# Block order, transpose placement, pairing and slot-table scatters in a fused decoder layer with 32 experts

## The chip, the cores and the metric

The kernel runs on one core of one Trainium2 chip. The metric is the device time of one execution in microseconds (us), lower is better. Shown are the median of three timed runs and one profiled execution.

## The reference, cut to what matters

One decoder layer for 1024 tokens of width 1024: a projection, banded attention and a convolution branch, their gated sum through `w_o`, a LayerNorm, and then a mixture of 32 experts of which each token takes four. The change touches the mixture alone:

```python
logits = h @ w_router + b_router
top_val, top_idx = lax.top_k(logits, TOP_K)         # 4 of 32
gates = softmax(top_val)
# the 4096 (token, expert) pairs are sorted by expert
for each expert e:
    up  = xb @ w_up[e] + b_up[e]                    # 1024 -> 2048
    act = min(glu, 7) * sigmoid(1.702 * glu) * (clip(lin, -7, 7) + 1)
    y  += gate * (act @ w_down[e] + b_down[e])      # 1024 -> 1024
x = layer_norm(alpha * h + y)
```

## The kernel before

**Dense part.** Up to about 640 us the kernel computes everything ahead of the experts. Its last loop runs over eight blocks of 128 tokens (lines 1120 to 1174): output projection, LayerNorm, router, top four, the rank of each token in its expert, and `place(b)` (line 1030), which writes for each of a token's four experts a record (token, gate) of 8 bytes into the slot table `tab` in HBM, by an indirect DMA from POOL. The token numbers of all records are written once (line 899). The framework orders two writes to `tab` by a wait for the first one's landing.

**Slot table and experts.** Experts are taken by rank of their token count; `CAPS` (line 52) gives each rank a fixed number of slots. A cap is cut into blocks of 128 (called F here), 64 and 32 slots: 320 is F, F, 64; 160 is F, 32; 96 is 64, 32. Tokens beyond a cap are counted by `overflow()` (line 1235, on DVE, called at slot 200) and worked off in a loop behind the last pair, which is skipped if there are none.

**Stages of an expert.** `fetch` reads its part of `tab`, `indices` turns it to integers, `gather` fetches the tokens' rows by indirect DMA into one of three buffers, and `x_T` (line 157) transposes them on TensorE (PE). A slot is a pair of weight tiles of 128 x 1024: slots 0 to 3 and 4 to 7 are the two halves of the up projection, 8 to 11 the down projection. `mm(s)` (line 233) runs the slot's products for every block, in order of the blocks. An F block takes 12 products of 128 x 512 a slot, each of high and low float32r parts of weights and inputs, which `split` (line 86) makes on ScalarE (ACT) and VectorE (DVE). Blocks of 64 and 32 take plain float32 products that use 64 or 32 columns of the array; in the trace each shows as two records. After slots 3 and 7 `swiglus` (line 281) adds the bias and applies the activation, on DVE and ACT, block by block. `act_T` (line 286) transposes the activations for the down projection. After slot 11 `scale_out` scales by the gate and `scatter` adds the rows to `yd` by indirect DMA. Sums stand in PSUM: five banks for sums (an F block takes two, a narrow one takes one) and three for transposes.

**Order of the work.** `PAIRS` (line 54) sets the order. A pair's slots interleave by fours: first expert 0 to 3, second 0 to 3, first 4 to 7, and so on, 24 slots a pair; the last pair runs one expert after the other. The list `G` holds all slots. The steps around them are put into a table `todo` by `at(slot, step)` (lines 1370 to 1409), and `behind(g)` (line 1411) issues those of slot g behind its products, in the order `rank_of`. `split_ahead` (line 1222) makes the high and low weights up to three slots ahead, and `load_ahead` loads weights from SP's queue as tile slots come free. POOL's queue carries, in program order, the scatters, table fetches, gathers and bias loads.

Of the kernel before, what the change touches and what calls it, by code (L numbers as in the profile page):

```python
# [15 lines left out]
ALU = mybir.AluOpType  # L16
# [7 lines left out]
NB = 8  # L24
# [25 lines left out]
BROW, BC, ACTB, XG = 2, 3, 3, 3  # L50
V_AT, S_AT = (2, 3, 4, 5, 7), (0, 3)
CAPS = [320, 288, 256, 256, 256, 256, 192, 192, 192, 160, 160, 160, 160, 128, 128, 128,
        128, 128, 128, 96, 96, 96, 96, 96, 96, 64, 64, 64, 64, 64, 64, 64]
PAIRS = [(6, 31), (1, 30), (13, 19), (2, 29), (9, 14), (7, 20), (21, 22), (0, 28), (15, 23), (3, 27), (10, 16), (8, 24),
         (11, 17), (4, 26), (12, 18), (5, 25)]
TR = 9 * P
FDVE = (0, 2, 5)

# [2 lines left out]
def kernel(ctx: ExitStack, tc: tile.TileContext, x, w_in, b_in, attn_sinks, w_attn_br,  # L61
# [39 lines left out]
    class Expert:  # L101
# [128 lines left out]
                        self.bias[u // 2, i, u % 2] = bc  # L230


        def mm(self, s, before=None):
            if s < 8 and s % 4 == 0 or s == 8:
                self.acc = [[acc(f"{self.pfx}{'d' if s == 8 else 'u'}{s}{i}{h}") for h in range(2 if w == P else 1)]
                            for i, (w, c) in enumerate(self.blocks)]
            raw, hi, lo = self.raw.pop(s), self.hi.pop(s, None), self.lo.pop(s, None)
            for i, (w, c) in enumerate(self.blocks):
                if before:
                    before(i)  # L240
                lhs = self.x[i] if s < 8 else self.aT[i]
                ng = P // w
                for kk in range(2):
                    k = 2 * (s % 4) + kk if s < 8 else 2 * (s - 8) + kk
                    st, sp = k == 0, k == KC - 1
                    if w == P and self.split:
                        terms = [(lhs[0], hi[kk]), (lhs[0], lo[kk]), (lhs[1], hi[kk])]
                    else:
                        terms = [(lhs[0], raw[kk])]
                    if w == P:  # L250
                        for h in range(2):
                            for j, (a, b) in enumerate(terms):
                                nc.tensor.matmul(self.acc[i][h], a[:, k, :], b[:, h * 512:(h + 1) * 512],
                                                 start=st and j == 0, stop=sp and j == len(terms) - 1)
                    else:
                        for j, (a, b) in enumerate(terms):
                            for g in range(ng):
                                if s < 8 and w == 32:
                                    rhs = b.rearrange("p (a f b t) -> p a b f t", a=2, b=2, t=2)[:, g // 2, g % 2]
                                else:  # L260
                                    rhs = b[:, g * 8 * w:(g + 1) * 8 * w]
                                nc.tensor.matmul(self.acc[i][0][g * w:(g + 1) * w, :8 * w], a[:, k, :], rhs,
                                                 start=st and j == 0, stop=sp and j == len(terms) - 1)
            wfree.extend(self.held.pop(s))

        def swiglu(self, v, i, h=0):
            w = self.blocks[i][0]
# [11 lines left out]
                                           op1=ALU.mult)  # L279

        def swiglus(self, v):
            for i, (w, c) in enumerate(self.blocks):
                for h in range(2 if w == P else 1):
                    self.swiglu(v, i, h)

# [49 lines left out]
    with ExitStack() as dctx:  # L335
# [559 lines left out]
        IDX = (rt.tile([P, NE, 4, 2], F32, name="slt"), rt.tile([P, NE, 4], I32, name="gi"),  # L895
               rt.tile([P, NE, 4], I32, name="si"))
        REC = wp.tile([P, NB, TOPK, 2], F32, name="rec", tag="rec", bufs=1)
        for b in range(NB):
            nc.gpsimd.tensor_scalar(REC[:, b, :, 0], prt.to_broadcast([P, TOPK]), float(b * P), None, op0=ALU.add)
        ids = rt.tile([1, NE], I32, name="ids")  # L900
        ids2 = rt.tile([1, NE], I32, name="ids2")
        nxi = rt.tile([1, 1], I32, name="nxi")
# [126 lines left out]

        def place(b):  # L1030
            for k in range(TOPK):
                nc.gpsimd.indirect_dma_start(out=tab[:, :], out_offset=bass.IndirectOffsetOnAxis(  # L1032
                    ap=DST[b][:, k:k + 1], axis=0), in_=REC[:, b, k, :], in_offset=None)

        def weigh(b):
            e4 = RG[b]
# [152 lines left out]
    with tc.manual_schedule():  # L1189
# [182 lines left out]

        blocks = [(e, i) for e in ex for i in range(e.nb)]
        g0 = {e.pfx: pos[e.pfx, 0] for e in ex}
        tpos = [g0[e.pfx] - 2 - e.nb + i for e, i in blocks]
        for n, e in enumerate(ex):
            p = g0[e.pfx] // 24 * 24
            if n > 1:
                at(p - 16, e.fetch)
                at(p - 13, e.indices)  # L1380
            for v in range(2):
                q = pos[e.pfx, 4 * v]
                at(min(q, g0[e.pfx] + 1) - 4 if e is last else q - 4, e.load_bias, v)
# [3 lines left out]
                at(q + 1, e.bias_of, 2 * v + 1)  # L1387
                at(q + 3, e.swiglus, v)
            for i in range(e.nb):
                at(pos[e.pfx, 4 + i], e.act_T, 0, i)  # L1390
                at(pos[e.pfx, 8 + (i > 0)], e.act_T, 1, i)
                if e is not last:
                    at(pos[e.pfx, 11], e.scale_out, i)
            if e is not last:
# [8 lines left out]
        for n, (e, i) in enumerate(blocks):  # L1403
            if n >= XG:
                f = g0[e.pfx] // 24 * 24
                at(max(tpos[n - XG], f - 12), e.gather, i)
        for n, (e, i) in enumerate(blocks):
            if e is not ex[0]:
                at(tpos[n], e.x_T, i)

        def behind(g):

            for f, a in sorted(todo.pop(g, ()), key=lambda fa: rank_of.index(fa[0].__name__)):
                f(*a)


        for g in range(FIRST):
# [13 lines left out]
        nc.vector.tensor_copy(bcol[:, 0, :], ccol[0:NE].to_broadcast([NE, P]))  # L1431
        for g, (e, s) in enumerate(G):
            split_ahead(g)
            e.mm(s, (lambda i: e.x_T(i) if i else None) if g == 0 else None)
            if g == 200:
                overflow()
            load_ahead(g)
# [65 lines left out]
```

## Time and profile before

| what | us |
|---|---|
| median of three runs | 2166.6 (2164.72 to 2170.33) |
| profiled execution | 2165.14 |
| its span on the core | 2163.5 |
| PE busy | 2064.2 |
| DVE busy | 1376.7 |
| ACT busy | 884.8 |
| POOL busy | 485.1 |

The span runs from the first instruction to the last. Busy time is the time in which an engine has at least one instruction at work; a list of waits gives the time in which it had none, with what ended each such time. The expert stage begins with the first transposes at 663.5 us. In the timeline a row has its start, its length, engine, line, operation, output <- inputs, the form of the array (rows * columns) and a count.

### The profile page before, as it was taken

The page shows a single profiled execution, that of the slowest core. Times are in us where ns is not written, and L with a number is a line of the kernel's source. Part 1 is how long each engine was busy: PE and PEld are TensorE (multiplying, and loading weights), DVE is VectorE, ACT ScalarE, POOL GpSimd, SP SyncE. Part 2 cuts the span into 40 slices and gives each one's busy share as a digit, 9 for nine tenths or more (in the row PEclk, how much of TensorE's full clock was granted, in tenths as well). Part 3 has the DMA queues.
Part 4 walks back from the last instruction along what each step waited for, and adds up shares of the span by engine and source line. Part 5 has one row for each costly group of instructions (what it writes and reads, how often), then busy time and mean ns, then how long its engine had stood idle before and what let it go on. Part 6 is the DMA issues. An engine that isn't in the chain of part 4 may idle for free. (4 is left out here: it accounts for less than half of the span.)

```text
span 2163.5 us, 31942 instructions
## 1 busy us (share of the span) xinstructions
PE 2064.2 (95%) x10929; PEld 1369.1 (63%) x10929; DVE 1376.7 (64%) x2058; ACT 884.8 (41%) x1356; POOL 485.1 (22%) x659
## 2 busy tenths in 40 slices
PE   7999999999977999999999999999999999999993
PEld 6776788887644566566664346556766456766771
DVE  3768799666765545654966134465678559649856
ACT  3155511432333424343653132333366346536633
POOL 1000000003324122322322332132141432322211
PEclk9999999999988999999999999999999999999997
DMA  6111011142237978998898997799889989997985
GB/s 199 42 39 30 20 54 54 44 133 62 99 136 261 334 262 296 376 349 302 276 313 298 341 362 248 263 321 374 306 263 316 329 264 323 346 313 259 333 288 214
DMA packets 191877, 510.84 MB, mean 236 GB/s; under 512 B 34844, under 2 KB 71118, under 8 KB 191709
## 3 DMA queue, kind: packets, MB, share of 16 engines
q1 hardware_dynamic: 162342, 446.76, 58.2%
q0 software_dynamic: 28816, 60.33, 10.9%
q8 instruction: 87, 1.43, 0.3%
q10 hardware_dynamic: 551, 1.66, 0.2%
q14 instruction: 81, 0.66, 0.1%
HBM read 473.08 MB, written 35.59 MB: 235 GB/s over the span
## 5 line engine op out<-in xcount | busy, mean ns | idle before, releaser
L611 DVE SCALAR_TENSOR_TENSOR c<-a,cw,c 128x1024 f32<-128x1024 f32 x120 | 154.0, 1284 | 3.3
L839 POOL DMA_DIRECT2D bu<-in_b_up_dram x2 | 1.0, 501 | 451.1 <-DVE wol L88 451.1
L141 POOL DMA_DIRECT2D slt<-tab x103 | 54.4, 529 | 30.4 <-issue 17.7
L91 PE MATMUL ga<-xh,whga 128*128 128x512 f32 x128 | 52.1, 407 | 0.0
L93 PE MATMUL ga<-xh,wlga 128*128 128x512 f32 x128 | 50.5, 395 | 0.0
L92 PE MATMUL ga<-xl,whga 128*128 128x512 f32 x128 | 50.5, 394 | 0.0
L93 PE MATMUL gb<-xh,wlgb 128*128 128x512 f32 x128 | 50.4, 394 | 0.0
L91 PE MATMUL gb<-xh,whgb 128*128 128x512 f32 x128 | 50.4, 394 | 0.0
L92 PE MATMUL gb<-xl,whgb 128*128 128x512 f32 x128 | 50.4, 394 | 0.0
L1032 POOL DMA_INDIRECT tab<-rec,dst x32 | 32.3, 1008 | 58.6 <-DMA tab<-rec,dst 55.8
L938 PE MATMUL wo<-woh,mh 128*128 128x512 f32 x128 | 36.9, 421 | 0.6 <-ACT mh L87 0.6
L938 PE MATMUL wo<-woh,ml 128*128 128x512 f32 x128 | 35.9, 404 | 0.0
L88 DVE TENSOR_TENSOR p7l<-p7w,p7h 128x1024 fp32r<-128x1024 f32 x24 | 29.5, 1279 | 9.6 <-ACT p7h L87 9.6
L88 DVE TENSOR_TENSOR p5l<-p5w,p5h 128x1024 fp32r<-128x1024 f32 x24 | 29.1, 1245 | 9.8 <-ACT p5h L87 9.1
L451 ACT ACTIVATE gt<-ga,pcol 128x512 f32<-128x512 f32 x16 | 11.0, 690 | 59.2 <-PE ga L93 59.1
L88 DVE TENSOR_TENSOR p8l<-p8w,p8h 128x1024 fp32r<-128x1024 f32 x24 | 28.5, 1241 | 10.1 <-ACT p8h L87 10.1
L654 DVE SCALAR_TENSOR_TENSOR sc<-s,mask 128x512 f32<-128x512 f32 (+1 forms) x32 | 19.5, 652 | 24.0 <-PE s L651 21.8
L88 DVE TENSOR_TENSOR p15l<-p15w,p15h 128x1024 fp32r<-128x1024 f32 x24 | 28.3, 1227 | 9.5 <-ACT p15h L87 9.4
L88 DVE TENSOR_TENSOR p13l<-p13w,p13h 128x1024 fp32r<-128x1024 f32 x24 | 29.0, 1257 | 8.4 <-ACT p13h L87 8.2
L88 DVE TENSOR_TENSOR p0l<-p0w,p0h 128x1024 fp32r<-128x1024 f32 x24 | 29.7, 1279 | 7.3 <-ACT p0h L87 7.1
L938 PE MATMUL wo<-wol,mh 128*128 128x512 f32 x128 | 33.9, 399 | 0.0
L88 DVE TENSOR_TENSOR p11l<-p11w,p11h 128x1024 fp32r<-128x1024 f32 x24 | 29.8, 1294 | 4.8 <-ACT p11h L87 4.6
(1271 smaller groups left out, 6373.0 us busy)
## 6 DMA issues: line engine op xcount, KB each, us to landing
p6w<-in_w_up_dram SPq DMA_DIRECT2D x16, 512.0 KB, 9.4
p31w<-in_w_up_dram SPq DMA_DIRECT2D x16, 512.0 KB, 8.3
p1w<-in_w_up_dram SPq DMA_DIRECT2D x16, 512.0 KB, 9.2
p30w<-in_w_up_dram SPq DMA_DIRECT2D x16, 512.0 KB, 5.4
p13w<-in_w_up_dram SPq DMA_DIRECT2D x16, 512.0 KB, 9.0
p19w<-in_w_up_dram SPq DMA_DIRECT2D x16, 512.0 KB, 13.2
p2w<-in_w_up_dram SPq DMA_DIRECT2D x16, 512.0 KB, 12.5
p29w<-in_w_up_dram SPq DMA_DIRECT2D x16, 512.0 KB, 11.5
```

The costliest lines, as they stand in the source:

```text
L88: nc.vector.tensor_tensor(lo, src, hi.bitcast(F32), op=ALU.subtract)
L91: nc.tensor.matmul(o, ah, bh, start=start, stop=False)
L92: nc.tensor.matmul(o, ah, bl, start=False, stop=False)
L93: nc.tensor.matmul(o, al, bh, start=False, stop=stop)
L141: nc.gpsimd.dma_start(self.m[g * w:(g + 1) * w, i, :], tab[bass.ds(row + c, w), :])
L451: nc.scalar.activation(GT[c][:, sl], t, AF.Sigmoid, bias=bin_c(14 + c))
L611: nc.vector.scalar_tensor_tensor(C[c], A[c][:, w:w + S], cw[:, c, w:w + 1], C[c], op0=ALU.mult, op1=ALU.add)
L654: nc.vector.scalar_tensor_tensor(SC[b][c0 // 2][:, g::2, :W], t[g][:, :, :W], 0.125, mk[:, None, :].to_broadcast([P, 2, W]), op0=ALU.mult, ...
L839: nc.gpsimd.dma_start(bu, b_up[:, i * S:(i + 1) * S])
L938: nc.tensor.matmul(t, ml[:, k, :], W[k][:, sl], start=n == 0, stop=n == 3 * KC - 1)
L1032: nc.gpsimd.indirect_dma_start(out=tab[:, :], out_offset=bass.IndirectOffsetOnAxis(ap=DST[b][:, k:k + 1], axis=0), in_=REC[:, b, k, :], in ...
```

## The change

The cap of rank 24 falls from 96 to 64. The pairs are chosen anew. In `mm` odd slots run the blocks in reverse; `between` lets the transposes due at an even slot run where it goes from F to narrow blocks. `swiglus` takes the blocks in reverse. Transposes of inputs move 3 slots earlier for the first expert of a pair; those of activations go to slots 5 and 8, and for a second expert without an F block 2 slots earlier. `fetch`, `indices` and `gather` move 4 to 5 slots earlier. `place` writes the token numbers itself, record by record, and its scatters are declared free of order among themselves.

```diff
 CAPS = [320, 288, 256, 256, 256, 256, 192, 192, 192, 160, 160, 160, 160, 128, 128, 128,
-        128, 128, 128, 96, 96, 96, 96, 96, 96, 64, 64, 64, 64, 64, 64, 64]
-PAIRS = [(6, 31), (1, 30), (13, 19), (2, 29), (9, 14), (7, 20), (21, 22), (0, 28), (15, 23), (3, 27), (10, 16), (8, 24),
-         (11, 17), (4, 26), (12, 18), (5, 25)]
+        128, 128, 128, 96, 96, 96, 96, 96, 64, 64, 64, 64, 64, 64, 64, 64]
+PAIRS = [(6, 31), (1, 30), (13, 19), (2, 29), (9, 14), (3, 28), (10, 15), (0, 27), (21, 22), (4, 26), (8, 20), (16, 23),
+         (11, 17), (7, 24), (12, 18), (5, 25)]
...
-        def mm(self, s, before=None):
+        def mm(self, s, before=None, between=None):
...
-            for i, (w, c) in enumerate(self.blocks):
+            order = list(range(self.nb))[::-1 if s % 2 else 1]
+            for n, i in enumerate(order):
+                w, c = self.blocks[i]
+                if between and n and s % 2 == 0 and w < P and self.blocks[order[n - 1]][0] == P:
+                    between()
+                    between = None
...
             wfree.extend(self.held.pop(s))
+            return between
...
         def swiglus(self, v):
-            for i, (w, c) in enumerate(self.blocks):
+            for i, (w, c) in reversed(list(enumerate(self.blocks))):
...
-        for b in range(NB):
-            nc.gpsimd.tensor_scalar(REC[:, b, :, 0], prt.to_broadcast([P, TOPK]), float(b * P), None, op0=ALU.add)
...
         def place(b):
             for k in range(TOPK):
-                nc.gpsimd.indirect_dma_start(out=tab[:, :], out_offset=bass.IndirectOffsetOnAxis(
+                nc.gpsimd.tensor_scalar(REC[:, b, k, 0:1], prt, float(b * P), None, op0=ALU.add)
+
+                i = nc.gpsimd.indirect_dma_start(out=tab[:, :], out_offset=bass.IndirectOffsetOnAxis(
                     ap=DST[b][:, k:k + 1], axis=0), in_=REC[:, b, k, :], in_offset=None)
+                tc.declare_no_dep(i.ins, group="place", reason="every token has a slot of its own")
+                tc.add_to_no_dep_group("place", i.ins)
...
-        tpos = [g0[e.pfx] - 2 - e.nb + i for e, i in blocks]
+        tpos = [g0[e.pfx] - (5 if n % 2 == 0 and n else 2) - e.nb + i for n, e in enumerate(ex) for i in range(e.nb)]
...
             if n > 1:
-                at(p - 16, e.fetch)
-                at(p - 13, e.indices)
+                at(p - 21, e.fetch)
+                at(p - 17, e.indices)
...
             for i in range(e.nb):
-                at(pos[e.pfx, 4 + i], e.act_T, 0, i)
-                at(pos[e.pfx, 8 + (i > 0)], e.act_T, 1, i)
+
+                d = -2 if n % 2 and e is not last and e.full == 0 else 0
+                at(pos[e.pfx, 4] + (d or (1 if e.nb > 1 else 0)), e.act_T, 0, i)
+                at(pos[e.pfx, 8] + (d or 0), e.act_T, 1, i)
...
-                at(max(tpos[n - XG], f - 12), e.gather, i)
+                at(max(tpos[n - XG], f - 16), e.gather, i)
...
-        def behind(g):
-
-            for f, a in sorted(todo.pop(g, ()), key=lambda fa: rank_of.index(fa[0].__name__)):
-                f(*a)
+        def behind(g, of=lambda f: True):
+
+            fs = sorted(todo.pop(g, ()), key=lambda fa: rank_of.index(fa[0].__name__))
+            todo[g] = [fa for fa in fs if not of(fa[0].__name__)]
+            if not todo[g]:
+                del todo[g]
+            for f, a in fs:
+                if of(f.__name__):
+                    f(*a)
...
-            e.mm(s, (lambda i: e.x_T(i) if i else None) if g == 0 else None)
+            between = e.mm(s, (lambda i: e.x_T(i) if i else None) if g == 0 else None,
+                           lambda: behind(g, lambda name: name in ("x_T", "act_T")))
+            if between:
+                between()
```

## Rows read from the trace of the kernel before

**Rows 1.** The page, busy us (share of the span) and instructions.

```profile
PE 2064.2 (95%) x10929; PEld 1369.1 (63%) x10929; DVE 1376.7 (64%) x2058; ACT 884.8 (41%) x1356; POOL 485.1 (22%) x659
```

**Rows 2.** Waits of PE: waiter <- releaser, us in total, times, longest.

```profile
PE fsp L1350 <- DVE fmvs L1348: 25.5, 1, 25.5
PE p6xt L167 <- DMA p6xg<-hd,gi: 20.0, 1, 20.0
PE p15u L253 <- DVE p15l L88: 4.5, 1, 4.5
...
PE p9d L253 <- DVE p9al L88: 0.8, 1, 0.8
```

**Rows 3.** Timeline of PE, pair (2, 29): first product of a plain run, and its end.

```profile
945.74 0.50 PE L253 MATMUL p2u<-p2h,p2xh 128*128 128x512 f32 x1
...
956.85 0.65 PE L262 MATMUL p29u<-p29w,p29xr 128*64 128x512 f32 x2
```

**Rows 4.** Timeline of PE, pair (6, 31): narrow and plain runs in turn.

```profile
681.59 1.94 PE L262 MATMUL p6u<-p6w,p6xr 128*64 128x512 f32 x8
683.46 0.50 PE L253 MATMUL p6u<-p6h,p6xh 128*128 128x512 f32 x1
...
686.44 1.94 PE L262 MATMUL p6u<-p6w,p6xr 128*64 128x512 f32 x8
...
695.18 0.50 PE L253 MATMUL p6u<-p6h,p6xh 128*128 128x512 f32 x1
```

**Rows 5.** Timeline of PE, pair (21, 22): three slots of 64 and 32 lie between.

```profile
1256.28 0.65 PE L262 MATMUL p22u<-p22w,p22xr 128*64 128x512 f32 x2
...
1264.97 0.39 PE L298 MATMUL p21aT<-ident,p21act 128*128 128x128 f32 x1
```

**Rows 6.** Timeline of PE, pair (21, 22): transposes between narrow products.

```profile
1278.16 1.09 PE L167 MATMUL p0xt<-ident,p0xg 128*128 128x128 f32 x8
```

**Rows 7.** Timeline of DVE and PE around the overflow count, pair (15, 23).

```profile
1436.11 0.18 DVE L1241 TENSOR_TENSOR over<-scnt_ps,capr 128x32 f32<-128x32 f32 x1
...
1442.53 0.17 DVE L1267 CAST xci<-xcol 128x2 int32<-128x2 f32 x1
...
1444.48 0.80 PE L253 MATMUL p15u<-p15l,p15xh 128*128 128x512 f32 x1 [4.48 <-DVE p15l L88]
...
1449.47 0.77 PE L262 MATMUL p23u<-p23w,p23xr 128*64 128x512 f32 x2
```

**Rows 8.** Window behind that wait: us, busy by engine, PEclk, DMA share, GB/s.

```profile
1444.50:1449.40 4.90, 4.90 (x11) 3.49 (x11) 2.06 (x3) 0.24 (x1) 0.00 (x0) 0.50 0.82 97
```

**Rows 9.** Timeline of DVE and POOL at the end of the dense part.

```profile
637.78 0.16 DVE L1027 SCALAR_TENSOR_TENSOR dst<-tif,rk 128x4 int32<-128x4 f32 x1
...
642.68 0.98 POOL L1032 DMA_INDIRECT tab<-rec,dst  x1 [5.76 <-DMA tab<-rec,dst]
...
651.66 0.97 POOL L1032 DMA_INDIRECT tab<-rec,dst  x1 [1.40 <-DMA tab<-rec,dst]
654.06 1.75 POOL L141 DMA_DIRECT2D slt<-tab  x3 [1.43 <-DMA tab<-rec,dst]
```

**Rows 10.** Windows by pair, (13, 19), (9, 14), (21, 22): PE, PEld, DVE, ACT, POOL.

```profile
859.64:933.96 74.32, 74.18 (x481) 42.00 (x479) 48.42 (x68) 35.18 (x50) 26.46 (x35) 1.00 1.04 373
1026.74:1115.30 88.56, 86.56 (x524) 62.08 (x523) 81.27 (x104) 58.20 (x75) 26.10 (x34) 1.00 0.85 290
1211.50:1288.93 77.43, 77.43 (x649) 27.14 (x645) 18.81 (x43) 14.95 (x31) 24.52 (x35) 1.00 1.04 353
```

**Rows 11.** Timeline of DVE, expert 0: the first operations of two halves of swiglu.

```profile
1314.69 0.69 DVE L272 TENSOR_TENSOR p0t<-p0u,p0bc 128x512 f32<-128x512 f32 x1 [17.67 <-PE p0u L253]
...
1316.73 0.69 DVE L272 TENSOR_TENSOR p0t<-p0u,p0bc 128x512 f32<-128x512 f32 x1
```

**Rows 12.** Waits of POOL, and what DVE's addition of p21's bias waited for.

```profile
POOL p13xg L154 <- DVE si L148: 33.2, 1, 33.2
...
  DMA p21bg<-bud: 9.3, 1
```

## The prediction

> **What bounds the kernel now.** I read the busy times first: TensorE (PE) is busy for 95% of the span [rows 1], so the next question is what it waits for. The list of its waits has few entries [rows 2]: 20.0 us for the first gather of the expert stage, 4.5 us in expert p15, and sub-microsecond waits on VectorE (DVE). (The 25.5 us at the end belong to the closing normalisation, which the change leaves alone.) From 663.5 us on PE simply works through its list, so there a change is worth what it takes off PE's list, wherever no other engine is close behind. So I then read the PE timeline for what one instruction costs and what a change of form costs (form: the shape in which the array is used, 128 output columns, 64, 32, or a transpose over 64 or 32 rows), and the stretches by pair of experts for who is close behind.
>
> **Prices.** In a plain run 48 products of 128 columns take 956.85 - 945.74 = 11.11 us [rows 3], 0.2315 each, 2.78 per slot of 12. Between narrow runs the same 12 take 686.44 - 683.46 = 2.98 [rows 4]: 0.20 more. A run of 8 narrow 64-column records (a float32 product shows as two) takes 1.87, and 40 take 8.74, so 32 more cost 6.87, 0.215 each; 8 alone would be 1.72, so a run carries 0.15 [rows 4]. Going to the narrow form and back costs 0.20 + 0.15 = 0.35, **0.175 us a change**. A slot of an expert with a 64 and a 32 block takes 8.69 / 3 = 2.90 [rows 5]; without 1.72 for its 64 block the 32 block and its two changes are 1.18, the block alone 0.83.
>
> **The change, part by part.**
>
> *Expert 24 loses its 32 block* (cap 96 to 64). 12 slots x 0.83 = 10.0 us, and some 1 us for 8 + 2 small transposes (an estimate: eight large ones take 1.09 [rows 6]). Its loads, scatter and 12 small DMAs lie beside other work. Gain 11. Tokens over a cap would run an extra pass after the last pair; the reference's routing sends 57 tokens to the 25th expert, so 64 suffice.
>
> *Turned order.* Odd slots run their blocks backwards, so F N, F N, F N, F N becomes F N, N F, F N, N F. I counted the changes of form between the matrix products from the two lists of pairs: before, pair by pair, 23, 27, 27, 6, 25, 44, 48, 24, 27, 6, 25, 44, 25, 5, 25, 1, together 382; after 17, 18, 18, 6, 13, 5, 13, 17, 24, 6, 30, 18, 13, 17, 13, 1, together 229. For example p9 (F and 32) beside p14 (F): 8 changes a phase become 4. 153 x 0.175 = 26.8 us.
>
> *Transposes.* A transpose of 128 rows is of the F form; inside a narrow run it costs two more changes. The partner's activations now go into the first expert's slots (2 slots earlier), the inputs 3 slots earlier. Counted the same way with the transposes in, the changes are 483 before and 293 after: 37 beyond the 153. 37 x 0.175 = 6.5 us. With x_T move its gather (16 instead of 12 slots ahead), the fetch of the slot table (21 for 16) and the index conversion (17 for 13): POOL issues the same instructions, now ahead of one phase more of bias loads. Their cost on PE is nothing as long as PE has products to run and the bias still comes in time; if not, each late microsecond is PE's (rival below). SP's weight loads keep their order; slots come free as before.
>
> *New pairs.* Slot 200, at which the overflow count is made, falls into the pair (21, 22) instead of (15, 23). The count keeps DVE from 1436.11 to 1442.7, with a weight split queued behind it; PE then waits 4.48 us, and the next 12 products take 1449.47 - 1444.48 = 4.99 instead of 2.78 [rows 7], at a granted clock of 0.50, the lower of the two levels, 1.2 GHz [rows 8]. (21, 22) has no F block and no split, so nothing is queued behind the chain: 4.5 + 2.2 = 6.7 us gained.
>
> *Scatters without order.* The last block's destinations are ready at 637.94, but its first scatter is issued at 642.68 and the fourth at 651.66, each after the one before has landed; the fetch follows at 654.06 [rows 9]. Unordered, each costs POOL 0.97 of issue and, as an estimate, 0.6 for the new small operation ahead of it and the semaphore: four are out by 644.4. A landing took 1.4 us in quiet and up to 5.8 beside the first weight loads [rows 9]; I take 2.5, nearer the quiet end since those loads are ending. Fetch at 647, 7 us earlier, and all that follows with it (fetch, indices, gather, first transpose) as PE has nothing else to do. Bounds 0 and 9. The order of the earlier blocks' scatters frees POOL only where PE doesn't wait for it.
>
> *Given back.* (a) In the four pairs of two F experts DVE is busy 81.3 of 88.6 us while PE is 86.6 [rows 10], and PE already waits for DVE there [rows 2]. 12 changes fewer, 2.1 us, put PE's need at 84.5 with DVE's unchanged, and DVE may split only three slots ahead; in the two up phases DVE is behind. I keep a third: -1.4 x 4 = -5.6 (bounds 0 and -8.4). (b) swiglus now takes the narrow block first and block 0 last. Experts 0 and 1 have three blocks and fill all five accumulator banks, so the partner's first product needs block 0's bank. One half takes DVE 1316.73 - 1314.69 = 2.04 [rows 11]; after the narrow block PE needs 2.98 + 2.78 = 5.8 to the end of the slot, and DVE comes to block 0 after three halves, from 0.1 + 2.0, then (waiting for block 1's first half) from 2.5 + 4.0 = 6.5, and frees the bank with its 0.7 us addition at 7.2: 1.4 us of wait, twice a pair, two pairs, 5.6. Should the pool hand out the bank that is released first, it is 0; with the same at the down phase 7. I take -5, nearest to what the round order of five banks gives. (c) (13, 19) and (21, 22) run at a DMA share of 1.04 [rows 10], so transfers can become late there: -1.
>
> **Sum.** 11 + 26.8 + 6.5 + 6.7 + 7 - 5.6 - 5 - 1 = 46.4. The profiled execution took 2165.1 (span 2163.5, 1.6 around it); the median of the runs is 2166.6, 1.5 above. 2165.1 - 46.4 = 2118.7, with the 1.5 added **2120 us**. About 0.3%, 6.5 us, is what a measurement of this kernel can tell from no change.
>
> **Rivals.**
>
> *Nothing is given back.* DVE and the banks keep up: 2120 - 11.6 = 2108. For it: DVE waits in the profile are under 1 us each [rows 2]; against it DVE's 92% in four pairs [rows 10].
>
> *Transfers pace the narrow pairs.* At 373 and 353 GB/s the engines of the narrow pairs are full [rows 10]; if PE was only just fed, (13, 19), (21, 22) and the new (16, 23) keep their lengths and lose what I gave them: 9, 24 and 9 changes x 0.175 and some 1 us of transposes each, 10 us, and DVE the rest of (a): 2120 + 10 + 2.8 = 2133. For it: share 1.04. Against: no wait of PE for a raw weight is in the list.
>
> *Slower: a late bias.* POOL works in order. Gathers now stand in the slot in which the second expert's bias is asked for, and a gather waits for indices: 33.2 us once [rows 12]. A bias row has already made DVE wait 9.3 us for p21 [rows 12], which cost PE nothing, since the partner's phase of 4 x 2.90 = 11.6 us covers it. From there each further microsecond stops PE for want of a bank. With the bias 16 us late in each of 15 pairs it would be 15 x 4.4 = 66: 2186. Against it: the second expert's bias is needed 7 slots, over 19 us, after it is asked for.
>
> *Slower: the clock.* Transposes now stand together, up to 13 in one slot. If such a batch let the clock fall, each would cost what the fall after the wait in p15 cost, 2.2 us [rows 7]; two batches a pair, 32 x 2.2 = 70: 2190. Against it: ten transposes in a row (8 at 1278.16 [rows 6], then 2) lie in a stretch with a granted clock of 1.00 [rows 10]. The Trainium skill, in "TensorE: Matmul & The Clock Gate", Part 4: PE-mode transpose, says that transposes do not count as PE activity in the way matmuls do, by which the batches could bring the clock down; the stretch just named does not agree.
>
> *The change doesn't do what it says.* If the scatters still wait for each other (through the tile they read, which is now written between them), the 7 us stay: 2127.
>
> **How the numbers follow.** Forecast 0.62 (2110 to 2129), nothing given back 0.15, transfers 0.13, scatters still ordered or little gained 0.05 (0.01 of it within 0.3%), late bias 0.03, clock 0.02. Faster 0.94, same 0.01, slower 0.05. The range, 2104 to 2136, takes in the bounds of the front (0 to 9), of (a) and (b), and the transfer case.
>
> **What would show it.** Right: narrow runs twice as long in p6 to p12; no wait in the ninth pair; last scatter and fetch 2 to 3 us apart, the first wait of PE near 13 us; the partners' 64 blocks without transposes inside their runs; (9, 14) shorter by about 1 us only; a wait of 1 to 1.5 us at the first products of p30 and p27. Wrong: PE waits for raw weights or for bias in the list, a clock below 1.00 between 700 and 2050 us, or plain F products slower than 0.23.

## The result and the profile after

| what | before | after |
|---|---|---|
| median of the runs, us | 2166.39 (2164.72 to 2170.33) | 2142.24 (2138.92 to 2142.89) |
| ratio, 95% interval | | 0.9883 (0.9869 to 0.9897) |
| span of the profiled execution | 2163.5 | 2141.3 |

The changed kernel is faster by 24 us, 1.2%; forecast were 46 and a time from 2104 to 2136. The direction was right, the size was not, and the time lies outside the range. (One execution of an experiment's kernel, e7, took 4305 us and is left out of its time below.) In the profiled executions the gain is 2163.5 - 2141.3 = 22.2 us. It has three parts, read one after the other: the front, the expert stage and the end.

The busy times, the packets of the software queue (q0; 28816 before) and the table fetches (103 before) on the page of after:

```profile
PE 2029.4 (95%) x10727; PEld 1377.7 (64%) x10727; DVE 1372.5 (64%) x2049; ACT 881.0 (41%) x1350; POOL 508.2 (24%) x669
...
q0 software_dynamic: 28240, 59.80, 11.1%
...
L141 POOL DMA_DIRECT2D slt<-tab x99 | 60.7, 876 | 15.0 <-DMA yd<-p15ys,gi 5.1
```

PE is busy 34.8 us less than before [rows 1], more than the 22.2 gained: some of its work went and idle time came. **The front**, timeline of DVE, POOL and PE:

```profile
635.37 0.16 DVE L1033 SCALAR_TENSOR_TENSOR dst<-tif,rk 128x4 int32<-128x4 f32 x1
...
639.53 1.06 POOL L1040 DMA_INDIRECT tab<-rec,dst  x1 [0.28 <-POOL rec L1038]
...
641.13 1.06 POOL L1040 DMA_INDIRECT tab<-rec,dst  x1 [0.28 <-POOL rec L1038]
...
645.22 1.74 POOL L141 DMA_DIRECT2D slt<-tab  x3 [3.03 <-DMA tab<-rec,dst]
...
653.73 1.94 PE L167 MATMUL p6xt<-ident,p6xg 128*128 128x128 f32 x8 [11.86 <-DMA p6xg<-hd,gi]
```

The last scatters are 1.6 us apart and wait only for the small operation ahead of them, not for a landing [rows 9]; the fetch stands at 645.22 instead of 654.06, and PE's wait for the first gather falls from 20.0 to 11.9 [rows 2]. The first transposes come 9.8 us earlier, at 653.73 instead of 663.48. Of these, 2.4 lie ahead of the scatters: the last block's destinations are ready at 635.53 instead of 637.94 [rows 9]. **The expert stage**, list of PE's waits:

```profile
PE fsp L1360 <- DVE fmvs L1358: 24.0, 1, 24.0
...
PE p6xt L167 <- DMA p6xg<-hd,gi: 11.9, 1, 11.9
PE p10aT L306 <- DVE p0xl L88: 6.7, 1, 6.7
...
PE p6aT L306 <- DVE p1xl L88: 2.0, 1, 2.0
...
PE p18u L260 <- ACT p18h L87: 1.6, 1, 1.6
...
PE p16d L260 <- ACT p16ah L87: 1.2, 1, 1.2
```

The 4.5 us for p15l are gone; two new waits stand in front, both of the activations' transposes for a split of *inputs* (p0xl, p1xl). The timeline of PE, DVE and ACT around the longer one:

```profile
1258.31 1.03 PE L167 MATMUL p0xt<-ident,p0xg 128*128 128x128 f32 x8
1259.18 0.64 PE L306 MATMUL p10aT<-ident,p10act 128*128 128x128 f32 x4
1259.42 0.68 DVE L280 TENSOR_TENSOR p15t<-p15u,p15bc 128x512 f32<-128x512 f32 x1
...
1262.39 2.00 ACT L87 ACTIVATE p10h<-p10w 128x1024 fp32r<-128x1024 f32 x2
...
1263.48 2.36 DVE L88 TENSOR_TENSOR p10l<-p10w,p10h 128x1024 fp32r<-128x1024 f32 x2
1264.28 1.07 ACT L87 ACTIVATE p0xh<-p0xt 128x512 fp32r<-128x512 f32 x2
...
1265.76 1.28 DVE L88 TENSOR_TENSOR p0xl<-p0xt,p0xh 128x512 fp32r<-128x512 f32 x2
1266.50 0.48 PE L306 MATMUL p10aT<-ident,p10act 128*128 128x128 f32 x1 [6.68 <-DVE p0xl L88]
1266.90 3.64 PE L269 MATMUL p10d<-p10w,p10ar 128*32 128x256 f32 x32
...
1278.45 1.92 PE L269 MATMUL p10d<-p10w,p10ar 128*32 128x256 f32 x30
```

The slot has four groups of transposes to do: two of x_T for expert 0 (two tiles of four), act_T of p10's F block and of its 32 block. There are three banks for transposes. The first three groups go through, the fourth needs a bank, and the bank is freed by the splits of p0's inputs, which stand on ACT and DVE behind p15's activation and p10's weight split. PE stands still for 6.68 us, and the narrow run behind it takes 3.64 where one of the same kind takes 1.92: the granted clock is 0.50 there, in a window just behind the wait:

```profile
1266.50:1270.50 4.00, 4.00 (x34) 1.56 (x34) 3.37 (x4) 2.17 (x3) 0.00 (x0) 0.50 0.34 79
```

Windows by pair of after, columns as in [rows 10]:

```profile
655.50:745.33 89.83, 86.67 (x394) 46.03 (x393) 51.45 (x72) 39.09 (x53) 25.92 (x34) 0.97 0.97 341
...
849.89:926.13 76.24, 73.76 (x481) 42.58 (x479) 46.77 (x66) 33.80 (x47) 25.48 (x34) 1.00 1.04 360
1018.34:1106.32 87.98, 85.77 (x524) 65.16 (x523) 80.92 (x102) 58.19 (x75) 23.43 (x28) 0.98 0.87 289
1198.36:1294.58 96.22, 87.88 (x532) 65.41 (x531) 81.68 (x103) 58.91 (x76) 33.95 (x33) 0.95 0.84 275
1409.88:1484.05 74.17, 73.39 (x627) 27.75 (x623) 23.23 (x76) 12.92 (x28) 19.87 (x29) 1.00 1.03 344
1671.51:1748.49 76.98, 74.74 (x480) 43.47 (x478) 46.10 (x64) 33.33 (x47) 29.34 (x41) 0.98 1.02 355
1835.65:1917.32 81.67, 81.67 (x378) 43.38 (x376) 46.50 (x64) 33.85 (x47) 22.75 (x30) 1.00 1.03 370
```

In order (6, 31), (13, 19), (9, 14), (10, 15), (21, 22), (16, 23), (7, 24). The first, second and fourth became longer than before (87.8, 74.3 and, for (10, 16), 88.7), (7, 24) is 15.8 shorter than (7, 20). **The end**, the last row of the timeline, after and then before:

```profile
2124.25 1.02 POOL L1371 DMA_INDIRECT out_dram<-yg,si  x1 [29.84 <-DVE yg L1368]
```

```profile
2157.30 1.03 POOL L1361 DMA_INDIRECT out_dram<-yg,si  x1 [30.12 <-DVE yg L1358]
```

It ends at 2125.27, the span at 2141.3: 16.0 us later. Before, the same row ended at 2158.33 and the span at 2163.5, 5.2 us later. So the last scatter came 33.1 us earlier, and 10.9 of these were lost behind it, where no view shows an instruction. The packed trace has two long records there, both of POOL: one named INC_SWDGE_SEM takes 2.69 us, 0.54 before, and the closing drain 10.20, 1.45 before. Together they are 10.9 longer, which is the whole loss.

### The profile page after: what moved, and what is told of

It is laid out like the page before. It is cut to its first block, busy times and chain, and to the rows that moved or that the text cites. A ratio compares the mean times of both kernels' runs of the same rounds, so it can differ in the third digit from the quotient of the medians.

```text
span 2141.3 us, 31584 instructions
## 1 busy us (share of the span) xinstructions
PE 2029.4 (95%) x10727; PEld 1377.7 (64%) x10727; DVE 1372.5 (64%) x2049; ACT 881.0 (41%) x1350; POOL 508.2 (24%) x669
## 5 line engine op out<-in xcount | busy, mean ns | idle before, releaser
L141 POOL DMA_DIRECT2D slt<-tab x99 | 60.7, 876 | 15.0 <-DMA yd<-p15ys,gi 5.1
L88 DVE TENSOR_TENSOR p16l<-p16w,p16h 128x1024 fp32r<-128x1024 f32 x24 | 29.3, 1261 | 18.7 <-ACT p16h L87 18.6
L1040 POOL DMA_INDIRECT tab<-rec,dst x32 | 36.6, 1143 | 15.5 <-POOL rec L1038 8.5
L88 DVE TENSOR_TENSOR p10l<-p10w,p10h 128x1024 fp32r<-128x1024 f32 x24 | 29.7, 1295 | 14.9 <-ACT p10h L87 14.8
L88 DVE TENSOR_TENSOR p8l<-p8w,p8h 128x1024 fp32r<-128x1024 f32 x24 | 28.5, 1242 | 15.8 <-ACT p8h L87 15.7
L88 DVE TENSOR_TENSOR p1l<-p1w,p1h 128x1024 fp32r<-128x1024 f32 x24 | 28.6, 1242 | 15.3 <-ACT p1h L87 15.2
L88 DVE TENSOR_TENSOR p9l<-p9w,p9h 128x1024 fp32r<-128x1024 f32 x24 | 28.8, 1257 | 14.2 <-ACT p9h L87 14.1
L88 DVE TENSOR_TENSOR p13l<-p13w,p13h 128x1024 fp32r<-128x1024 f32 x24 | 28.8, 1239 | 14.2 <-ACT p13h L87 14.1
L88 DVE TENSOR_TENSOR p12l<-p12w,p12h 128x1024 fp32r<-128x1024 f32 x24 | 28.8, 1258 | 13.1 <-ACT p12h L87 12.9
L88 DVE TENSOR_TENSOR p2l<-p2w,p2h 128x1024 fp32r<-128x1024 f32 x24 | 28.2, 1222 | 12.8 <-ACT p2h L87 12.4
L88 DVE TENSOR_TENSOR p4l<-p4w,p4h 128x1024 fp32r<-128x1024 f32 x24 | 28.2, 1222 | 12.9 <-ACT p4h L87 10.9
```

The costliest lines, as they stand in the source:

```text
L88: nc.vector.tensor_tensor(lo, src, hi.bitcast(F32), op=ALU.subtract)
L141: nc.gpsimd.dma_start(self.m[g * w:(g + 1) * w, i, :], tab[bass.ds(row + c, w), :])
L1040: i = nc.gpsimd.indirect_dma_start(out=tab[:, :], out_offset=bass.IndirectOffsetOnAxis(ap=DST[b][:, k:k + 1], axis=0), in_=REC[:, b, k, :] ...
```

## The experiments

Lengths of the pairs in the profiled executions, from the first product of one pair to that of the next (us; before's partner in brackets where it differs; the kernels are told of below):

| pair | before | after | e2 | e3 | e5 | e9 |
|---|---|---|---|---|---|---|
| (6, 31) | 87.8 | 89.8 | 85.6 | 86.9 | 87.0 | 90.9 |
| (1, 30) | 106.6 | 104.6 | 104.6 | 106.2 | 106.5 | 105.7 |
| (13, 19) | 74.3 | 76.2 | 75.5 | 75.0 | 73.6 | 76.3 |
| (2, 29) | 92.8 | 92.2 | 92.2 | 92.8 | 92.8 | 92.2 |
| (9, 14) | 88.7 | 88.0 | 87.3 | 86.9 | 87.1 | 87.4 |
| (3, 28) [3, 27] | 92.8 | 92.0 | 92.0 | 92.7 | 92.6 | 92.0 |
| (10, 15) [10, 16] | 88.7 | 96.2 | 88.4 | 88.9 | 90.1 | 98.8 |
| (0, 27) [0, 28] | 116.7 | 115.3 | 115.3 | 116.9 | 116.8 | 116.0 |
| (21, 22) | 76.0 | 74.2 | 74.3 | 74.2 | 73.9 | 76.3 |
| (4, 26) | 92.6 | 92.2 | 92.2 | 92.9 | 92.8 | 92.2 |
| (8, 20) [8, 24] | 97.7 | 95.2 | 95.2 | 96.2 | 96.3 | 97.5 |
| (16, 23) [15, 23] | 82.2 | 77.0 | 77.7 | 76.7 | 75.4 | 77.8 |
| (11, 17) | 88.9 | 87.2 | 87.4 | 87.9 | 90.1 | 89.8 |
| (7, 24) [7, 20] | 97.5 | 81.7 | 81.7 | 82.8 | 82.9 | 82.7 |
| (12, 18) | 88.7 | 88.3 | 87.7 | 87.8 | 89.2 | 90.5 |

**e1, the scatters alone**: the edit of `place` from the diff above, in the kernel before.

> The kernel before with the slot table's scatters unordered and nothing else. In the changed kernel the first transposes of the expert stage start 8.9 us earlier (654.60 instead of 663.48), but the span ends 16.0 us behind the last scatter's issue (2124.25+1.02 to 2141.3) instead of 5.2 (2157.30+1.03 to 2163.5). Theory A, the long end comes from something in the expert stage or from how much POOL has done: here the first transposes start at about 654.6, all after it as before, the end stays near 5 us, and the time is 2166.4 - 8.9 = 2157.5. Rival B, the long end comes with the unordered scatters: the end is 15 to 16 us here too, and the time is 2157.5 + 10.9 = 2168, no change. Rival C, the pull at the front is lost again within the first pair, as its weights or gathers come late: the first transposes early, but the start of the pair (1, 30) at 753 as before, and the time near 2166.

Ratio 0.9971 (0.996 to 0.9982), 6.3 us; first transposes at 654.37, end 5.0 us, (1, 30) from 743.9 on instead of 753.0. Theory A holds: the front is worth about the 7 that were forecast, and the long end does not come with it.

**e2, three-block inputs one slot later.**

```diff
-        tpos = [g0[e.pfx] - (5 if n % 2 == 0 and n else 2) - e.nb + i for n, e in enumerate(ex) for i in range(e.nb)]
+        tpos = [g0[e.pfx] - (5 if n % 2 == 0 and n else 2) - min(e.nb, 2) + i for n, e in ...
```

> The changed kernel, but the input transposes of the experts with three blocks (0 and 1) begin one slot later, behind the slot in which the other expert's activations are transposed. Theory: PE's waits of 6.7 us (p10aT for p0xl) and 2.0 us (p6aT for p1xl), both new, come from four transposes' tiles in one slot with three banks for them, and the clock fell behind each (the next narrow run 3.6 for 1.95, and 5.3 for 3.6). Then both waits go, (10, 15) falls from 96.2 to about 87.5 and (6, 31) from 89.8 to about 86.5, and the time from 2142 to about 2130. Rival: VectorE is the bound in (10, 15), so the wait only moves to the next products that need a split: (10, 15) stays above 93 and the time above 2138.

2131.43, ratio 0.9855 (0.984 to 0.9869); the profiled execution is 12.6 shorter than after's. Windows of (6, 31) and (10, 15):

```profile
656.97:742.61 85.64, 84.80 (x393) 45.89 (x393) 50.71 (x72) 38.78 (x53) 25.29 (x34) 0.98 1.00 355
1194.23:1282.64 88.41, 85.84 (x532) 64.30 (x531) 80.30 (x102) 58.24 (x76) 33.55 (x33) 1.00 0.89 297
```

As the theory had it, both waits are gone, the two pairs are 4.2 and 7.8 shorter, 12.0 together, and the granted clock of (10, 15) is 1.00 instead of 0.95. It was the banks, not DVE's load: DVE is nearly as busy as in the changed kernel (80.3 for 81.7 us). The 13 transposes that stood in one row are now 5 and 8, in two slots.

**e3, activations back; e5, all transposes back.** In both, `at` gets back its old slots (4 + i, 8 + (i > 0)), and `between` lets only `x_T`, or nothing, through; e5 has the offset 2 for the inputs, too.

> The changed kernel with the activations' transposes back where the kernel before has them (inside the narrow runs); the input transposes stay in their new place. By the prediction's price (0.175 us a change of form, and two changes for a transpose in a narrow run) 57 changes come back, 10 us: with the wait at p10aT gone (four tiles no longer stand in one slot; 9 with the clock behind it) and that at p6aT (4), 2142 - 13 + 10 = 2139. Theory: a transpose inside a narrow run costs its own time only, since the narrow runs of (13, 19) take 11.64 us net of transposes with and 11.63 without them; then nothing is paid and the waits go, also those for p13al, p16ah and p16al: (13, 19) falls from 76.2 to about 73, and the time is about 2126.

> The changed kernel with all transposes, inputs and activations, back where the kernel before has them: only the turned order, the pairs, the smaller cap and the unordered scatters are left. By the prediction's price 483 - 382 - (293 - 229) = 37 changes come back, 6.5 us, against 12.4 us of new waits and lower clock that go: 2142 - 12.4 + 6.5 = 2136. Theory (transposes in narrow runs cost nothing more, and the moved ones brought the new waits on ACT and DVE in (6, 31), (13, 19), (10, 15) and (16, 23)): about 2142 - 12.4 - 5 = 2125. In both the three-block experts' banks could make p30 and p27 wait (1.4 us each phase), which the changed kernel did not show.

e3: 2140.51, ratio 0.9895 (0.988 to 0.9909). e5: 2142.65, 0.9917 (0.9901 to 0.9932); its executions spread from 2138.76, the profiled one, to 2152.27. The theory (a transpose in a narrow run costs nothing more) fell: with e5 seven pairs, (1, 30), (2, 29), (3, 28), (0, 27), (4, 26), (8, 20) and (7, 24), are 7.5 us longer together.

The count of changes in the two expectations is too low. Counted in the traces in the way of the prediction, transposes included, before has 483, the changed kernel 293, e3 390 and e5 394: 97 and 101 come back, not 57 and 37. In the turned order the narrow blocks of two slots meet, and a transpose in its old place cuts their run in two; in the straight order most stood at the end of a narrow run, where the form changed anyway. In the seven pairs 54 changes come back, 0.14 us each, a little less than the prediction's 0.175.

In (13, 19) and (16, 23) e5 is 2.6 and 1.6 *shorter* than after. That is a hint that there the moved transposes cost more than they give, and no more: (16, 23) took 77.7 in e2 and 73.4 in e6 (below) with the same list of products and transposes.

**e7, a mix** for these two pairs: the next inputs go back to their old slots, p19's and p23's activations to slots 5 and 8 of their own expert (before, 4 and 5, 8 and 9), all else as e2.

> The kernel of e2, but beside p13 and p16 (one F block each) the partner's activations (p19, p23) and the next expert's inputs (p2, p11) go back to the old slots. With all transposes old (e5), (13, 19) took 73.6 instead of 75.5 and (16, 23) 75.4 instead of 77.7, while seven other pairs were 0.6 to 1.9 us longer each. Theory: in these two pairs the F time is short, so the transposes that are moved into it find ACT and DVE with weight splits and swiglu to do (p13al, p16ah, p16al), and in the narrow time they wait for nobody: (13, 19) about 73.6, (16, 23) about 75.4, the time 2131.4 - 4 = 2127.5. Rival: what the two pairs gain comes back in (2, 29) and (11, 17), whose inputs are late again (1 to 2 us): 2130 to 2131.

2135.64, ratio 0.9867 (0.9848 to 0.9886); (13, 19) took 77.1 and (16, 23) 80.2, longer than in e2. Both theory and rival failed: moving these transposes back did not shorten the two pairs. As the activations are not quite in their old slots, e7 is not e5's placement for these pairs.

**e9, straight order.** The two reversed orders, that of the products' blocks and that of `swiglus`, taken out of the changed kernel.

> The changed kernel with the blocks in straight order in every slot, and swiglus from the first block on, as before; pairs, caps, transposes and scatters stay changed. 360 instead of 229 changes of form between products. By the prediction's price 131 x 0.175 = 22.9 us more, of which the three or four pairs of two F experts give little (DVE): 2139 + 17 to 23 = 2156 to 2162. Rival: in the pairs in which the changed kernel gained nothing ((13, 19), (21, 22), (16, 23)) something other than the form paces them, so the order is worth half or less: below 2151. In either case the waits of p10aT and p6aT should stay or move by little.

2154.61, ratio 0.9941 (0.9927 to 0.9956): 12.6 us by the ratios, 14.1 in the profiled executions from the first transposes to the last scatter, not 17 to 23. The 131 changes of the expectation are those between products; with the transposes in, the trace has 411 changes, 118 more than the changed kernel. By the table: 2.6, 2.6 and 2.2 in three pairs of two F experts and -0.6 in the fourth, for 12 changes each; 2.3 for 14 in (8, 20), 1.1 for 8 in (1, 30), 2.1 for 16 in (21, 22), where only 64 and 32 blocks alternate, but 0.1 and 0.8 for 9 each in (13, 19) and (16, 23).

**e8, expert 24's cap at 96 again**, in the changed kernel (one number of `CAPS`).

> The changed kernel with expert 24's cap at 96 again, nothing else. On this step the prediction put 11 us of TensorE time; with the form changes of its narrow runs 13. On a chip where before takes 2164, the changed kernel takes 0.9883 of it, 2139. Theory A (the long end comes with the fewer transfers of the smaller cap, as the count of software packets is 28816 again here): (7, 24) grows from 81.7 to 94 or 95, the end falls from 16 to 5, and the time is 2139 + 13 - 11 = 2141, so the smaller cap as a whole gave 2 us of its 13. Rival B: the end stays at 16: 2152.

2147.86, ratio 0.9916 (0.9903 to 0.993). (7, 24) takes 94.9, 13.2 more, and the end is 5.0:

```profile
2138.31 1.04 POOL L1371 DMA_INDIRECT out_dram<-yg,si  x1 [29.80 <-DVE yg L1368]
```

(span 2144.3). Pair and end are as theory A has them, the time is above its 2141. The smaller cap saves 13 us on PE and loses 11 behind the last instruction. That leaves 2; the profiled spans differ by 3.0, and the ratios by 7, where each ratio has an interval of 3 us to either side.

**e6, e10, e12, e13: the count of software transfers.** e6, e10 and e12 are e2 with 14, 7 and 2 more small transfers on POOL's queue, e13 is the changed kernel with 7.

```diff
+        def pad(j):
+            nc.gpsimd.dma_start(spare[:32, 2 * j:2 * j + 2], tab[0:32, :])
+        for j in range(14):
+            at(75 + j, pad, j)
```

> The kernel of e2 (three-block inputs one slot later) with 14 more small software transfers in the pair (2, 29): 32 rows of the slot table into a tile that nobody reads. All kernels with the new caps end 15.9 to 16.0 us behind their last scatter, the kernel before and e1 with the old caps 5.0 to 5.2. The page gives 28816 packets on the software queue q0 before and 28240 after, 1801 and 1765 for each of 16 engines. Theory A: the end depends on where this count stands when the program ends; 14 transfers of one data and one semaphore packet an engine bring 1765 to 1793, near the old place: the end is about 5 us and the time 2131.4 - 10.9 = 2120.5. Rival B: the end belongs to another part of the change (pairs, order, earlier fetches): it stays at 16 and the time at 2131 to 2133. Rival C: another place in the count gives yet another length, longer or shorter than both.

> The kernel of e6 with 7 instead of 14 of the small software transfers: 494 transfers issued by POOL, 28464 packets. The end behind the last scatter was 5.0 to 5.2 us in the four kernels with 501 transfers and 15.8 to 16.0 in the six with 487, whatever else differed (packets 28816 and 28688 gave the same). Theory A: the end grows with each transfer that is missing to a full place in the count, 10.9 / 14 = 0.78 us each: here 5.2 + 7 x 0.78 = 10.6, the time 2123. Rival B: there is only one step somewhere between the two counts: 5 or 16 us, 2118 or 2129. Rival C: not the count decides, but what the transfers did to the last ones' timing: anything else.

> The kernel of e6 with 2 instead of 14 small transfers: 489 transfers issued by POOL. The end behind the last scatter was 15.9 to 16.0 us with 487 transfers, 4.3 with 494, 5.0 to 5.2 with 501 and 5.5 with 508: it falls once between 487 and 494 and then rises by about 0.1 us a transfer. If the fall lies between 487 and 489: about 3.8 us, the shortest of all. If it lies between 489 and 494: 16.1 us. Anything between, 8 to 13 us, would speak for a steep slope and against one fall.

> The changed kernel itself with 7 small software transfers added in the pair (2, 29), nothing else: 494 transfers. If the end's length hangs on this count alone, the end falls from 16.0 to 4.3, and the changed kernel's 0.9883 of the time before becomes 0.9883 - 11.7 / 2165 = 0.9829, 2128 where before takes 2165; the waits of p10aT and p6aT (6.7 and 2.0) stay. If the end was shortened by something that came with the moved inputs of e2, it stays at 16 and the ratio at 0.988.

The last scatter's row in e6 (span 2116.0), e10 (2113.2), e12 (2126.1) and e13 (2130.8):

```profile
2109.77 1.02 POOL L1371 DMA_INDIRECT out_dram<-yg,si  x1 [30.55 <-DVE yg L1368]
```

```profile
2107.86 1.03 POOL L1371 DMA_INDIRECT out_dram<-yg,si  x1 [27.13 <-DVE yg L1368]
```

```profile
2109.17 1.02 POOL L1371 DMA_INDIRECT out_dram<-yg,si  x1 [29.89 <-DVE yg L1368]
```

```profile
2125.21 1.02 POOL L1371 DMA_INDIRECT out_dram<-yg,si  x1 [26.89 <-DVE yg L1368]
```

| transfers issued by POOL | kernels | end behind the last scatter, us | POOL's closing drain, us |
|---|---|---|---|
| 487 | after, e2, e3, e5, e7, e9 | 15.8 to 16.0 | 10.20 |
| 489 | e12 | 15.9 | 10.36 |
| 494 | e10, e13 | 4.3, 4.6 | 0.88 |
| 501 | before, e1, e6, e8 | 5.0 to 5.2 | 1.45 |
| 508 | e11 | 5.5 | 2.03 |

e6: 2117.69, ratio 0.978 (0.9767 to 0.9792). e10: 2118.21, 0.9793 (0.9777 to 0.981). e12: 2129.64, 0.9838 (0.981 to 0.9865). e13: 2132.38, 0.9848 (0.9828 to 0.9867). The count decides, not what else differs: e6 and e8 have 28688 and 28816 packets and the same drain. Of e10, theory A fell; B had the one step right, but there is a slope beside it: the end rises by about 0.1 us a transfer and falls once between 489 and 494. e13 shows it for the changed kernel itself: seven idle transfers more, the end 11.5 us shorter, the time some 8 us by the ratios (its first transposes happened to come at 657.4; 652.1 to 657.4 in the profiles with unordered scatters). e6 and e10 are the fastest kernels of this study that load all weights, 22 and 19 us faster than the changed one by the ratios.

**e11, half of p19's and p23's weights**, on e6 with 21 small transfers.

```diff
+                if h and self.pfx in ("p19", "p23"):
+                    nc.sync.dma_start(self.wslot(s, f"w{s}{h}")[:, 0:8], w_up[bass.ds(ev, 1), 0:P, 0:8])
+                    self.raw[s].append(self.raw[s][0])
+                    continue
```

> The kernel of e6 with 21 small transfers (508 in all), and the second half of the weights of experts 19 and 23 is not loaded (8 columns of it are): their products read the first half twice, so 6 MB each of (13, 19) and (16, 23) move less. The end: by theory A of e10 the count passes the full place, so the end is as long as it can get, or still near 5 if 501 was not the full place but beside it; a step only (B) gives 5. The pairs: (13, 19) took 73.6 to 77.1 and (16, 23) 73.4 to 80.2 in the kernels so far with nearly the same list of instructions, at a DMA share of 1.02 to 1.04. Theory T, transfers pace the two pairs (ACT's weight split waited for p13w): with a quarter of the bytes gone (13, 19) falls to 72 to 73 and (16, 23) to 72 to 73, the sum below 146. Rival D, the in-order queues of ACT and DVE pace them: (13, 19) stays at 75 to 76, the sum above 148.

2115.68, ratio 0.9778 (0.9762 to 0.9795). Windows of (13, 19) and (16, 23):

```profile
845.61:920.11 74.50, 73.16 (x481) 42.73 (x479) 46.02 (x66) 33.94 (x47) 26.67 (x34) 1.00 0.94 298
1656.84:1729.28 72.44, 72.40 (x480) 42.43 (x478) 46.08 (x64) 33.67 (x47) 29.95 (x41) 1.00 0.91 297
```

The sum, 146.9, lies between the two theories: (16, 23) fell to where theory T had it, (13, 19) not as far. (16, 23) is the shortest of all kernels and has no wait of PE left; but in e6, with all weights, it took 73.4 and (13, 19) 75.7, so a quarter of the bytes is worth only 1.0 and 1.2. (13, 19) keeps two waits, 0.83 for p13al and 0.52 for p19ar. The run does not tell the theories apart; what makes (16, 23) swing between 73.4 and 80.2 stays open.

## Why the prediction was wrong, point by point

*Expert 24's block: right on PE, wrong behind it.* Priced at 11, with its form changes 13; e8 measured 13.2. The failed step is the sentence that its loads, scatter and 12 small DMAs "lie beside other work". They do, but 14 transfers fewer moved the program to another place of the count, and the end grew by 10.9 us. No row of before could show that; that the stretch behind the last row is 5.2 us long and belongs to nobody could be seen.

The Trainium skill, in "Runtime: NRT & Kernel Launch", section "The ~15µs preamble/postamble breakdown", lists a barrier with the reset of the DMA rings, together about 2 us, among the steps behind a kernel. No run here shows whether that step is part of this stretch, which took 4.3 to 16.0 us by the count of transfers.

*Transposes: the count of changes was right, what shares the slot was not looked at.* The traces have the 483 and 293 changes that were counted. Where PE is on its own (seven pairs, e5), a change is worth 0.14 us of the 0.175 priced. (By its own rows the price would even be 0.20: the plain run of [rows 3] has a change at either end, and between them the products start 0.227 apart.) The step that failed is the claim that moving the transposes costs nothing on PE "as long as PE has products to run": four groups for three banks, with the eviction queued on ACT and DVE behind swiglu and weight splits, cost 12.0 us (e2). The prediction followed the moved steps past POOL's queue, but not through the PSUM banks that they share.

*The rival on the clock: its sign came, its cause is not borne out.* A granted clock below 1.00 between 700 and 2050 us was named as a sign of being wrong. There are four such stretches, at 719, 1071, 1262 and 1729 us, and each begins in or right behind waits of PE: the 2.0 us for p1xl, 1.0 and 0.8 in (9, 14), the 6.7 us for p0xl, 1.2 and 0.8 in (16, 23). The 0.97 of (6, 31) also holds the end of the wait for the first gather. Rows of transposes without such a wait leave the clock at 1.00; the longest is one of 12, in the kernel before (timeline and window):

```profile
1104.98 1.03 PE L167 MATMUL p7xt<-ident,p7xg 128*128 128x128 f32 x8
1105.86 0.64 PE L298 MATMUL p14aT<-ident,p14act 128*128 128x128 f32 x4
...
1104.00:1114.00 10.00, 10.00 (x55) 8.18 (x55) 8.77 (x10) 8.12 (x11) 4.34 (x5) 1.00 1.02 350
```

The changed kernel's rows of 13 and 14 have the long waits inside them, and e2 takes away row and wait together, so no run has such a row without a wait. The rule of the Trainium skill weighed there ("TensorE: Matmul & The Clock Gate", Part 4) is not borne out by rows of up to 12; the falls follow the waits.

*Turned order: near its price.* The 131 changes between products that it saves among the new pairs were priced at 22.9 or, less (a), 17.3. With the transposes in, e9 has 118, which is 20.7 or, less (a), 15.1; it found 12.6 to 14.1. Some of what is missing lies in (13, 19) and (16, 23), where 18 changes gave 0.9 us.

*Transfers in the narrow pairs: (c) was too small.* This is the third step that failed: (c) gave back 1 us for (13, 19) and (21, 22). By the prediction's price and the changes in the traces (13, 22 and 11 fewer), with the 6.7 us of the overflow count, (13, 19), (21, 22) and (16, 23) should have gained 2.3, 3.9 and 8.6 us; they gained -1.9, 1.9 and 5.2 (from unrounded lengths), together 9.6 less. The rival had the right place, and with its 10 us the right size. What shows on PE is that it stands still for 2.5, 0.8 and 2.2 us of the three pairs' windows after, for splits and for copies out of PSUM; before, it was 0.1 in (13, 19) and nothing in (21, 22) [rows 10]. That makes some 5.4 of the 9.6. The cause is not settled. The list of PE's waits has no raw weight, as the forecast argued against the rival, but ACT's list of waits in (13, 19) has one:

```profile
ACT p13h L87 <- DMA p13w<-in_w_down_dram: 1.8, 1, 1.8
```

A weight that comes late for ACT's split would show on PE as a wait for a split (p13l, p13al, p16ah), not for the transfer; that is argued, not shown. e11 gave only about 1 us for a quarter of the bytes, and in e6 (16, 23) took 73.4 with all of them, so the bytes alone do not settle it.

*Overflow count: right.* Nothing waits for it in (21, 22), and the 4.5 us are gone. *Scatters: right*, 6.3 by e1's ratio. From the last block's destinations to the first transposes it is 25.5 us before, 19.1 in e1 and 18.2 after, 6.4 and 7.3 less. The rest of the 9.8 lies ahead of them; the destinations came at 632.7 to 638.8 in the profiles with unordered scatters, so it may be chance. *(a): right*: (9, 14), (11, 17), (12, 18) are 0.7, 1.7 and 0.4 shorter with DVE at 80.9 of 88.0 us. *(b): did not come.* The timeline of PE and DVE where p30 begins:

```profile
772.26 0.39 PE L260 MATMUL p1u<-p1h,p1xl 128*128 128x512 f32 x1
...
772.58 7.09 PE L269 MATMUL p30u<-p30w,p30xr 128*64 128x512 f32 x32
...
773.61 0.68 DVE L280 TENSOR_TENSOR p1t<-p1u,p1bc 128x512 f32<-128x512 f32 x1
```

p30's first product follows p1's last at once, before DVE has read either half of p1's block 0 (the row at 773.61 is the first of them): it got another bank. Of the prediction's cases for (b), 0, 5 and 7, it was 0.

The sum in profiled executions: 46.4 forecast; (b), 5, not paid; 2.8 more at the front; 10.9 lost at the end, 12.0 to the banks: 31.3. Measured are 22.2. Of the other 9.1, 8.6 are what the three narrow pairs fell short by beyond (c). The terms at the front and of (b) that came out better hide 7.8 us of what the three failed steps cost.

## What to carry to other kernels

When work leaves a program, look also at what lies behind its last instruction: the span's end against the last row, before and after, is one subtraction. When steps are moved into one slot, count the tiles that they take from a shared pool and follow who frees each, through every in-order queue on the way. And count changes of form over the whole list, transposes included, for each order: what moving the transposes saves was 37 in the forecast's split and 101 once the order was turned. Where transfers or splits nearly fill a stretch as well, as in the three narrow pairs, such a price is an upper bound.

## What the runs showed of the hardware

The time from POOL's last scatter to the end of the span goes with the number of transfers that POOL has issued: 15.8 to 16.0 us at 487 and 489, 4.3 to 4.6 at 494, then rising with 501 and 508 to 5.5. POOL's drain rises by 0.57 us for 7 transfers, 0.082 each, from 494 to 508, and by 0.16 for 2 from 487 to 489, the same slope. If it keeps that slope over the whole height of 10.36 - 0.88 us, the pattern would repeat every 120 transfers or so (an estimate from these numbers; no run went through a whole period). With INC_SWDGE_SEM it is 0.10 a transfer. What POOL does in that time the trace does not show.
